# Renumbering the 128 slots of an expert's token tile: which partition holds which token

## The chip, the cores and the metric

The kernel runs on one core of one Trainium2 chip. The metric is device time in microseconds of one execution. Three runs of the kernel before took 906.35, 906.56 and 908.56 us, median 906.56.

## The reference

One decoder layer over 1024 tokens of width 1024, all float32: an input projection feeds sliding-window attention and latent attention, both go through one output projection, and a mixture of experts follows. What matters here is the last part:

```
expert_ids = g_idx * 8 + e_idx                      # best group of 4, best 2 of its 8 experts
combine    = weights placed at expert_ids           # (T, 32), two entries per token
hid = silu(x @ w_gate[e]) * (x @ w_up[e])           # for every expert e
hid = hid * combine[:, e]
out = sum over e of hid @ w_down[e]                 # then layer norm of ALPHA * h + out
```

So each of 1024 tokens goes to two of 32 experts: 2048 pairs, 64 an expert on average.

## The kernel before, in words

Everything up to the router runs in blocks of 128 tokens and ends at about 506 us of the span. The router (`route`) gives each pair of a token and an expert a running position p within that expert, in order of tokens. For a position below 128 it builds a one-hot row with `V.tensor_scalar(O, iota, pos[:, b, k:k + 1], None, op0=OP.is_equal)` (line 1529) and multiplies it on TensorE into a table `T` of 128 slots by 32 experts. So a pair with position p gets the slot s for which `iota[s] == p`. `finish_table` turns the table into `idxX` (the token's row for each slot, past the bound for an empty slot) and `wsl` (its weight). A slot is a partition of all the tiles that follow. Tile 24 in the order of work is an overflow tile, for an expert with more than 128 tokens, whose table `overflow_table` builds from the same `iota` (line 1843).

The expert stage then walks through 33 tiles of 128 slots. `gather_x` reads the 128 rows of a tile from `h1_d` by an indirect DMA of GpSimd (tile `w`), four tiles ahead of their use. `x_tr` transposes them on TensorE (`tr`), and `split` makes a high part on ScalarE (`xh`) and a low part on VectorE (`xl`). `gate_up` multiplies them by the expert's weights in four pieces (`gu`, three matmuls each: high by high, low by high, high by low), `hidden` makes `sil` and `hid`, `hid_tr` transposes and splits these (`hh`, `hl`), and `down` makes `y` in two halves, which ScalarE copies to a `w` tile. `scatter` adds its rows to `y_d` in DRAM by an indirect DMA of GpSimd with addition.

An expert's weights are three loads of 1024 KB each, 128 partitions of 8 KB, issued by SyncE into a ring of twelve buffers (tags `rw`, `rx`, `rv`, `rb`). A buffer comes free when `w_split` has made its two halves: `whg`, `whd` on ScalarE and `wlg`, `wld` on VectorE. `load_next` then issues the next load, so the ring holds the weights of four tiles.

After the last but two tiles the rows of `y_d` are read back (`z_load` by blocks, `old_rows` for the last two tiles by indirect DMA), normed and stored. `renorm` then writes the tokens of the last two tiles once more, by indirect DMA to the output.

The order of the instructions on each engine is set when the program is built: all operations are recorded, and `Sched.flush` puts them into order by a cost model of its own. Each engine works through its list in order. All operations are issued from one line, 312, so the names of tiles tell them apart in the profile.

Of the kernel before, what the change touches and what calls it, by code (L numbers as in the profile page):

```python
# [37 lines left out]
C_ID, C_TRI, C_IOTA, C_E32 = 0, 128, 256, 384  # L38
# [1933 lines left out]
def _constants():  # L1972
    import numpy as np
    c = np.zeros((128, C_END), np.float32)
    q = np.arange(128)[:, None]
    k = np.arange(128)[None, :]
    c[:, C_ID:C_ID + 128] = np.eye(128)
    cur = np.where(k <= q, 0.0, NEG)
    mask = np.concatenate([(k > q) & (k >= 128 - NMETA), cur, q > k, q <= k], axis=1).astype(np.float32)
    c[:, C_TRI:C_TRI + 128] = q < k  # L1980
    c[:, C_IOTA:C_IOTA + 128] = k % 8 * 16 + k // 8
    col = np.arange(512)[None, :]
    bd = ((q[:64] // NMETA) == (col // 128)).astype(np.float32)
    c[:, C_E32:C_E32 + 32] = np.arange(32)
    J, e = np.divmod(np.arange(224), 32)
    key = np.zeros((128, 2, 7, 32), np.float32)
    key[:, 0] = (32 * (J + 1) + e).reshape(7, 32)
    key[:, 1] = (128 * (J + 1)).reshape(7, 32)
    c[:, C_TOK:C_TOK + 8] = np.arange(128)[:, None] + 128 * np.arange(8)[None, :] - EMPTY
    c[:, C_WROW] = 3 * np.arange(128)  # L1990
    inv = 10000.0 ** (-np.arange(0, 64, 2, dtype=np.float32) / np.float32(64))
    pos = np.zeros((128, 9), np.float32)
    pos[:, :8] = NMETA + 128 * np.arange(8)[None, :] + np.arange(128)[:, None]
    pos[:, 8] = np.maximum(np.arange(128) - (128 - NMETA), 0)
    ang = (pos[:, :, None] * inv.astype(np.float32)[None, None, :]).astype(np.float32)
    rope = np.zeros((128, 9, 2, 64), np.float32)
    rope[:, :, 0, :32] = rope[:, :, 0, 32:] = np.cos(ang)
    rope[:, :, 1, :32] = -np.sin(ang)
    rope[:, :, 1, 32:] = np.sin(ang)
    return c, rope, bd, key, mask  # L2000
# [51 lines left out]
```

## Time and profile before

| | |
|---|---|
| median of three runs | 906.56 us |
| the profiled execution | 908.6 us |
| its span, first to last instruction | 906.7 us |
| TensorE busy | 802.8 us (89%) |
| VectorE busy | 686.1 us (76%) |
| ScalarE busy | 516.8 us (57%) |
| GpSimd busy | 310.6 us (34%) |
| queue of SyncE (hardware) | 36688 packets, 166.41 MB |
| queue of GpSimd (software) | 12816 packets, 28.87 MB |

A span is counted from the first instruction of the program, and all times below are on that clock. The expert stage lies between about 508 and 850 us. Busy shares are averages over stages with different limits, so the stage itself has to be read: the pace of its tiles, the time from a load's issue to its landing, and what stands ahead of each gap of TensorE. A load's landing is the time from the issuing instruction until the last of its sixteen engines has reported; with several loads in flight it holds the time in the queue too.

### The profile page before, as it was taken

Reading aid. Unit: us, or ns where it says so; the run is one execution under the profiler, and the core shown is the slowest. Engines: PE = TensorE matmul, PEld = TensorE weight load, DVE = VectorE, ACT = ScalarE, POOL = GpSimd, SP = SyncE. Lnnn points to the kernel's source line nnn. Section 1 sums busy time; section 2 is a strip of 40 time slices with the busy share of each in tenths; the row PEclk is TensorE's granted clock in tenths of the full one; section 3 lists DMA queues with packets and bytes.
Section 4 is the critical chain, followed back from the end, with each engine's and each line's share of the span. In section 5 each row is a group of like instructions: output and inputs, shape, how many; then the busy total and the mean of one; then the engine's idle time right before and its main releaser. Section 6 shows DMA issues by size and latency. Waiting matters only on the chain. (4 is left out here: it accounts for less than half of the span.)

```text
span 906.7 us, 13670 instructions
## 1 busy us (share of the span) xinstructions
PE 802.8 (89%) x4616; PEld 693.8 (77%) x4616; DVE 686.1 (76%) x1379; ACT 516.8 (57%) x966; POOL 310.6 (34%) x561
## 2 busy tenths in 40 slices
PE   3899999999999999999999599999999779989410
PEld 2798998999999988888887488888888658877310
DVE  7946623888777655758767799999999678979395
ACT  3524422576655645512122499999998578878351
POOL 3757423344331225223213414334343412321200
PEclk9999999999999999999999599999999979999855
DMA  9544512122211112699958469999999999994532
GB/s 333 173 152 160 177 68 92 35 87 69 84 51 47 48 70 70 218 343 411 350 170 308 150 222 362 353 373 370 354 356 329 357 328 346 366 317 131 177 141 105
DMA packets 49576, 196.17 MB, mean 216 GB/s; under 512 B 12688, under 2 KB 14224, under 8 KB 37344
## 3 DMA queue, kind: packets, MB, share of 16 engines
q1 hardware_dynamic: 36688, 166.41, 49.4%
q0 software_dynamic: 12816, 28.87, 11.5%
q8 instruction: 37, 0.61, 0.3%
q14 instruction: 35, 0.29, 0.1%
HBM read 165.57 MB, written 49.05 MB: 237 GB/s over the span
## 5 line engine op out<-in xcount | busy, mean ns | idle before, releaser
L312 POOL DMA_INDIRECT y_d<-w,idx x33 | 67.2, 2035 | 213.6 <-ACT w L312 184.7
L312 PE MATMUL sc<-wh,ht 128*128 128x448 f32 (+3 forms) x400 | 115.8, 370 | 1.9 <-DVE ht L312 1.3
L312 PE MATMUL gu<-whg,xh 128*128 128x512 f32 x264 | 110.2, 417 | 0.0
L312 PE MATMUL gu<-whg,xl 128*128 128x512 f32 x264 | 106.0, 402 | 0.7 <-DVE xl L312 0.7
L312 PE MATMUL gu<-wlg,xh 128*128 128x512 f32 x264 | 105.9, 401 | 0.0
L312 DVE TENSOR_TENSOR wlg<-rw,whg 128x1024 fp32r<-128x1024 f32 x80 | 96.4, 1221 | 12.3 <-ACT whg L312 11.7
L312 ACT ACTIVATE whg<-rw 128x1024 fp32r<-128x1024 f32 x80 | 83.8, 1062 | 23.4 <-PE gu L312 11.5
L312 PEld LDWEIGHTS sc<-wh,ht 128*128 128x128 f32 x400 | 73.8, 191 | 9.5 <-DVE ht L312 1.8
L312 PE MATMUL sc<-wl,ht 128*128 128x448 f32 (+3 forms) x200 | 72.8, 364 | 0.0
L312 PEld LDWEIGHTS gu<-whg,xl 128*128 128x128 f32 x264 | 50.9, 193 | 11.2 <-DVE xl L312 1.9
L312 DVE TENSOR_TENSOR wld<-rw,whd 128x1024 fp32r<-128x1024 f32 x46 | 54.4, 1221 | 6.5 <-ACT whd L312 6.4
L312 PEld LDWEIGHTS gu<-wlg,xh 128*128 128x128 f32 x264 | 50.7, 192 | 10.9
L312 PEld LDWEIGHTS gu<-whg,xh 128*128 128x128 f32 x264 | 51.1, 193 | 9.4 <-ACT xh L312 0.2
L312 PE MATMUL y<-whd,hh 128*128 128x512 f32 x124 | 52.0, 420 | 6.9 <-ACT hh L312 6.8
L312 POOL DMA_INDIRECT w<-h_d,idx x33 | 47.7, 1444 | 22.5 <-DMA y_d<-w,idx 11.0
L312 PE MATMUL tr<-cs,w 128*128 128x128 f32 x264 | 40.8, 279 | 12.9 <-DMA w<-h_d,idx 7.3
L312 PE MATMUL y<-whd,hl 128*128 128x512 f32 x124 | 50.2, 405 | 1.9 <-DVE hl L312 1.9
L312 PE MATMUL sc<-w,oT 128*128 128x512 f32 x192 | 49.8, 402 | 0.6 <-DMA oT<-o_d 0.6
L312 PEld LDWEIGHTS tr<-cs,w 128*128 128x128 f32 x264 | 33.6, 144 | 21.6 <-DVE wld L312 7.5
L312 PE MATMUL y<-wld,hh 128*128 128x512 f32 x124 | 49.6, 400 | 0.0
L312 ACT ACTIVATE pt<-sc,ng 128x272 f32<-128x272 f32 (+9 forms) x56 | 29.9, 538 | 34.5 <-DVE ng L312 34.3
L312 DVE TENSOR_TENSOR xl<-tr,xh 128x512 fp32r<-128x512 f32 x66 | 45.3, 687 | 3.9 <-ACT xh L312 3.7
(328 smaller groups left out, 2093.6 us busy)
## 6 DMA issues: line engine op xcount, KB each, us to landing
rw<-in_w_e_dram SPq DMA_DIRECT2D x64, 1024.0 KB, 24.5
rv<-in_w_e_dram SPq DMA_DIRECT2D x14, 1024.0 KB, 21.5
o_d<-oT SPq DMA_DIRECT2D x16, 512.0 KB, 2.8
oT<-o_d POOLq DMA_DIRECT2D x16, 512.0 KB, 8.5
rx<-in_w_e_dram SPq DMA_DIRECT2D x7, 1024.0 KB, 24.3
rb<-in_w_e_dram SPq DMA_DIRECT2D x7, 1024.0 KB, 26.2
x<-in_w_in_dram SPq DMA_DIRECT2D x8, 672.0 KB, 5.8
u_d<-r SPq DMA_DIRECT2D x7, 672.0 KB, 3.3
```

The source lines that it names most:

```text
L312: inst = getattr(t.eng.real, method)(*[self.real(a) for a in args], **{k: self.real(v) for k, v in kw.items()})
```

## The change

The 128 numbers of `iota` are permuted, and nothing else differs. Partition k stood for position k mod 8 x 16 + k div 8. Now it stands for the position whose lowest bit is bit 6 of k, whose bits 1 to 3 are bits 2 to 4 of k, whose bit 4 is bit 5 of k and whose bits 5 and 6 are bits 0 and 1 of k. Positions 0, 1, 2, 3 lay in partitions 0, 8, 16, 24; they lie in 0, 64, 4, 68 now. By the author's account partition bits 6 and 4 to 2 name a DMA engine, and successive rows are to lie on different engines.

```
@@ -1978,7 +1978,7 @@
     cur = np.where(k <= q, 0.0, NEG)
     mask = np.concatenate([(k > q) & (k >= 128 - NMETA), cur, q > k, q <= k], axis=1).astype(np.float32)
     c[:, C_TRI:C_TRI + 128] = q < k
-    c[:, C_IOTA:C_IOTA + 128] = k % 8 * 16 + k // 8
+    c[:, C_IOTA:C_IOTA + 128] = k // 64 + (k // 4 % 8) * 2 + (k // 32 % 2) * 16 + k % 4 * 32
     col = np.arange(512)[None, :]
     bd = ((q[:64] // NMETA) == (col // 128)).astype(np.float32)
     c[:, C_E32:C_E32 + 32] = np.arange(32)
```

On all five engines the instructions and their order are the same before and after. What differs is in the data: which slots of a tile are empty, and which partition a token's row is read into and added from.

## Rows read from the trace of the kernel before

**Rows 1.** Span and mean granted TensorE clock of the core.
```profile
core 0: 906.7 us, clock 0.948
```
**Rows 2.** Busy time by engine (PE, PEld, DVE, ACT, POOL), clock, DMA share, GB/s.
```profile
500.00:520.00 20.00, 8.72 (x30) 6.77 (x30) 15.22 (x47) 8.34 (x11) 9.77 (x8) 0.51 0.48 160
...
540.00:560.00 20.00, 20.00 (x99) 16.46 (x98) 19.43 (x22) 18.13 (x26) 7.45 (x5) 1.00 0.99 343
...
640.00:660.00 20.00, 20.00 (x100) 16.50 (x99) 19.83 (x25) 18.42 (x27) 9.13 (x5) 1.00 1.00 363
...
720.00:740.00 20.00, 12.48 (x47) 9.59 (x46) 11.43 (x14) 11.11 (x15) 6.37 (x5) 0.74 0.90 317
740.00:760.00 20.00, 16.99 (x76) 13.57 (x75) 14.89 (x17) 14.41 (x21) 3.44 (x3) 0.91 1.02 341
```
**Rows 3.** Issues at 526–537, 610–630, 685–705, 760–780: count, size, median us to landing.
```profile
rw<-in_w_e_dram SPq DMA_DIRECT2D x4, 1024.0 KB, 4.9
...
rw<-in_w_e_dram SPq DMA_DIRECT2D x4, 1024.0 KB, 23.2
...
rw<-in_w_e_dram SPq DMA_DIRECT2D x5, 1024.0 KB, 34.6
...
rw<-in_w_e_dram SPq DMA_DIRECT2D x4, 1024.0 KB, 25.1
```
**Rows 4.** ScalarE in order of time: start, us, operation, [idle before <- what ended it].
```profile
606.84 0.37 ACT L312 ACTIVATE sil<-gu 128x256 f32<-128x256 f32 x1
...
616.22 0.36 ACT L312 ACTIVATE sil<-gu 128x256 f32<-128x256 f32 x1
...
702.00 0.36 ACT L312 ACTIVATE sil<-gu 128x256 f32<-128x256 f32 x1
...
711.97 1.06 ACT L312 ACTIVATE whg<-rw 128x1024 fp32r<-128x1024 f32 x1 [2.66 <-DMA rw<-in_w_e_dram]
...
713.41 0.38 ACT L312 ACTIVATE sil<-gu 128x256 f32<-128x256 f32 x1
...
725.65 2.00 ACT L312 ACTIVATE whg<-rw 128x1024 fp32r<-128x1024 f32 x2 [6.17 <-DMA rw<-in_w_e_dram]
...
728.62 2.00 ACT L312 ACTIVATE whg<-rw 128x1024 fp32r<-128x1024 f32 x2 [0.70 <-DMA rw<-in_w_e_dram]
...
731.00 0.37 ACT L312 ACTIVATE sil<-gu 128x256 f32<-128x256 f32 x1
...
741.92 0.36 ACT L312 ACTIVATE sil<-gu 128x256 f32<-128x256 f32 x1
```
**Rows 5.** Waits, 520 to 800 us: total us, times, longest us.
```profile
ACT whg L312 <- DMA rw<-in_w_e_dram: 10.5, 4, 6.2
```
**Rows 6.** TensorE and ScalarE at two gaps of TensorE, as rows 4.
```profile
727.97 0.80 PE L312 MATMUL y<-whd,hh 128*128 128x512 f32 x1 [6.80 <-ACT hh L312]
...
747.46 0.66 PE L312 MATMUL tr<-cs,w 128*128 128x128 f32 x4 [2.87 <-DVE hl L312]
...
743.60 2.01 ACT L312 ACTIVATE whd<-rw 128x1024 fp32r<-128x1024 f32 x2
...
745.97 0.40 ACT L312 ACTIVATE hh<-tr 128x256 fp32r<-128x256 f32 x1
```
**Rows 7.** The same columns as rows 2, a stretch before the expert stage.
```profile
410.00:420.00 10.00, 10.00 (x66) 8.95 (x65) 8.12 (x34) 3.00 (x6) 2.96 (x10) 1.00 1.03 417
```
**Rows 8.** The first gather's landing, and the first transpose upon it.
```profile
w<-h_d,idx POOLq DMA_INDIRECT x1, 5.1
...
513.79 1.94 PE L312 MATMUL tr<-cs,w 128*128 128x128 f32 x8 [7.30 <-DMA w<-h_d,idx]
```
**Rows 9.** Landings of two late scatters, and the re-read of GpSimd behind the first.
```profile
y_d<-w,idx POOLq DMA_INDIRECT x1, 8.9
...
851.28 1.05 POOL L312 DMA_INDIRECT w<-y_d,idx  x1 [5.70 <-DMA y_d<-w,idx]
...
out_dram<-w,idx POOLq DMA_INDIRECT x1, 2.7
```

More of the change, by code (lines that the diff above doesn't have):

```diff
@@ L1980, in _constants @@
     c[:, C_TRI:C_TRI + 128] = q < k
-    c[:, C_IOTA:C_IOTA + 128] = k % 8 * 16 + k // 8
+    c[:, C_IOTA:C_IOTA + 128] = k // 64 + (k // 4 % 8) * 2 + (k // 32 % 2) * 16 + k % 4 * 32
     col = np.arange(512)[None, :]
```

## The prediction

> **What bounds the kernel now.** I read the span first [rows 1], then the expert stage in stretches of 20 us, then the landings of the weight loads there, then ScalarE's and TensorE's rows where TensorE stands still. In the stretches [rows 2] the pairs are busy microseconds and instruction counts of TensorE, its weight loads, VectorE, ScalarE and GpSimd; then come the granted clock, the DMA share and GB/s. From 540 to 680 TensorE is busy for 20.00 of 20 us at clock 1.00: the stage runs at TensorE's pace. A tile (one expert) takes 9.38 us there, from one `sil` to the next, 606.84 to 616.22 [rows 4]. But the DMA share is about 1.00 at some 360 GB/s, and behind this calm something runs out. A 1 MB weight load lands 4.9 us after its issue at 526 to 537, 23.2 us at 610 to 630, 34.6 us at 685 to 705, and 25.1 us at 760 to 780 [rows 3]. The twelve buffers hold four tiles, 4 x 9.38 = 37.5 us of work, so a landing of 34.6 us is the end of the cover. There ScalarE waits for `rw`: 2.66 us at 711.97, 6.17 at 725.65, 0.70 at 728.62 [rows 4], with one small wait more 10.5 us in four waits [rows 5]. It works in order, so the `hh` queued behind waits too, and TensorE loses 6.80 us before 727.97 [rows 6] and then its clock: 0.74 in 720 to 740, 0.91 in 740 to 760 [rows 2].
>
> So until 700 the stage is bound by TensorE, and its weight supply is slower than TensorE; about 710 to 742 it pays the debt.
>
> **The change, step by step.** No instruction is added, removed or moved; only the numbers in `iota` differ. They decide in which partition of a 128-slot tile an expert's p-th token lies, and so which partitions hold the real rows of each row gather and scatter-add; the empty slots have an index past the bound and move no row.
>
> *Step 1, the load on the DMA engines.* The change's own account takes a partition's bits 6 and 4 to 2 as the number of its DMA engine: sixteen engines, eight partitions each. The old numbering puts row p in partition (p mod 16) x 8 + p div 16. For p under 64 the last three bits are 0 to 3, so bit 2 is always 0: 64 rows lie on eight engines, eight on each, and the other eight engines get rows only from p = 64 on. The new numbering sends the low four bits of p to bits 6 and 4 to 2: 64 rows are four on each of sixteen. An expert gets 2048 / 32 = 64 rows on average; routing the reference's inputs gives 13 to 132. Summed over the first 20 tiles, the fullest engine has 6.7 rows a tile by the old numbering and 4.05 by the new one (mean 3.66).
>
> In bytes: a tile's weights are three loads of 1024 KB, 196.6 KB an engine. A row is 4 KB, moved once in and once out, 8.2 KB. The fullest engine has 196.6 + 6.7 x 8.2 = 251.5 KB a tile before and 196.6 + 4.05 x 8.2 = 229.8 after, 0.914 of it. If the adding scatter's read of its target counts too, 12.3 KB a row, it is 279.0 and 246.4, 0.883.
>
> *Step 2, the pace of the supply.* From the middle of 526 to 537 to that of 685 to 705 are 164 us, 17.5 tiles, and the landing grows by 34.6 - 4.9 = 29.7 us [rows 3], 1.7 us a tile. The crowded engines need 9.38 + 1.7 = 11.1 us a tile. As a check: eight engines at 251.5 KB per 11.1 us and eight at about 205 KB per 9.38 us are 181 + 175 = 356 GB/s, and the stretches show 343 and 363 [rows 2]. Afterwards 11.1 x 0.914 = 10.1, or x 0.883 = 9.8 us a tile; growth 0.4 to 0.8 us a tile. In 20 tiles the landing then reaches 13 to 20 us, in 32 tiles 18 to 29: under 34.6 throughout. No wait for weights is left, even if a third of the relief is missing.
>
> [...]
>
> *Step 3, what the waits were worth.* The three tile times that hold them are 702.00 to 713.41, to 731.00, to 741.92 [rows 4]: 11.41 + 17.59 + 10.92 = 39.92 us, against 3 x 9.38 = 28.14. That is 11.8 us, lost clock included. Bounds: 10.5 us if only ScalarE's waits go [rows 5]; nothing if the supply does not change; 14.7 if the 2.87 us gap at 747.46 goes as well [rows 6]. I take 11.8. That gap I leave standing: ahead of 747.46 TensorE waits for a transpose bank that is freed by `hh` and `hl`, and on ScalarE these stand behind two `whd` from 743.60, which run without a pause [rows 6]. It is the written order, no DMA, and the order stays. What is late next in 710 to 742 is TensorE itself, as in 540 to 680.
>
> *Step 4, the first gather.* It lands after 5.1 us and TensorE starts 513.79 upon it [rows 8]. The first tile has 66 rows: eight on a crowded engine before, at most five after. Three rows of 4 KB at 251.5 KB per 11.1 us are 0.5 us. Bounds: 0, if the clock, 0.51 in 500 to 520 [rows 2], rises no earlier; 2.4, if it lands like the 2.7 us scatter of 35 rows at the end [rows 9]. I take 0.5.
>
> *Step 5, the tail.* The scatter issued at 841.48 takes 8.9 us, and the re-read at 851.28 waits for it, 5.70 us of GpSimd's time [rows 9]. It has 93 rows, eight on an engine before and six after: two rows in and out at the same rate, 0.7 us; bounds 0 and 5.7. The last scatter [rows 9], of 35 rows, goes from five to three on an engine: 0.3 us at most. I take 0.7 for the two, since loads and VectorE's sums lie behind.
>
> *The hidden ones.* The other 32 gathers and 31 of the scatters land sooner as well, at no gain: a gather is issued four tiles ahead, and a `y_d` write is only read in the tail.
>
> Sum: 11.8 + 0.5 + 0.7 = 13.0 us. The profiled execution took 908.6 us (span 906.7), 2.0 over the median of the runs, 906.56. Against its own time the sum gives 895.6. If the 2.0 us is the profiled run's own, the median becomes 893.6; if it is a longer weight wait, which now goes, 895.6. I take **894.5**.
>
> **Rivals.**
>
> *A. It is the memory, not the engines.* If the 343 to 363 GB/s is what memory gives, all engines are slowed alike, evening them out does nothing, and steps 4 and 5 alone remain: 906.56 - 1.2 = 905.4. The same time comes if indirect rows are dealt by other bits, say partition modulo 16: the fullest engine then goes from 7.95 to 7.5 rows a tile, 0.1 us, 2 us in 20 tiles, 904.5. For it: the flat rate at a DMA share of 1.00. Against it: in 410 to 420, with whole 128-partition tiles only, the same core moves 417 GB/s at a share of 1.03 [rows 7]; and 66 rows, 0.27 MB, land in 5.1 us [rows 8] where a full 1 MB load with nothing queued before it takes 4.9 [rows 3], as rows crowded onto few engines would.
> [...]
>
> *B. Half.* The even load meets another limit on the way, and a tile's supply stays near 10.9 us. The landing grows 1.5 us a tile, the waits come three tiles later and half as long: 906.56 - 6 - 1 = 899.6. For it: the rate of the crowded engines, 251.5 KB per 11.1 us, is 22.7 GB/s, and sixteen at that rate are 362 GB/s, under the 417 of [rows 7], so something besides crowding slows them.
>
> *C. Slower.* If an indirect row's engine is its partition's block of eight (bits 6 to 3), the old numbering was the even one, 4.05 rows on the fullest engine, and the new one, whose bits 6 to 3 carry bits 0, 4, 3 and 2 of p, has 4.55. Half a row more is 4.1 KB of 229.8, 0.2 us of 11.1 a tile. At 711.97 the cover is spent, so every further microsecond of debt is waited for: 20 x 0.2 = 4 us, 910.6. It decides from 0.14 us a tile on (2.7 us). For it: nothing in the rows excludes an even load before. Against it: the same two points as against A.
>
> *D. More.* The two late gaps shrink too, since ScalarE comes to them earlier: 894.5 - 6 = 888.5. Against: at 743.60 it is the order that holds `hh` back.
>
> **How the numbers follow.** The forecast has 0.68 (its own range 890 to 898), A 0.08, B 0.12, C 0.06, D 0.06. The range 889 to 902 leaves out A, C, most of D and the upper end of B, under 2 in 10. About 0.3%, 2.7 us, is what a measurement of this kernel tells from no change: faster is under 903.8. That is the forecast, D and 0.10 of B: 0.84. The same: A and 0.02 of B, 0.10. Slower: C, 0.06.
>
> **What would show it.** Step 2: weight loads issued at 685 to 705 land in 13 to 20 us instead of 34.6, and GB/s in 640 to 660 rises from 363 to 364 to 375 (16 x 229.8 KB in 10.1 to 9.8 us). Step 3: no wait of ScalarE for `rw`, and `sil` rows 9.4 us apart through tiles 19 to 22, clock 1.00; the gap before the late transposes still there. Step 4: the first transpose at about 513.3. Step 5: the last big scatter in about 8 us. If landings still climb to 30 us, A or B is right; if they climb faster than 1.7 us a tile, C.

## The result, and the profile after

The kernel after takes 891.94 us (median of four runs, 891.67 to 893.8), the kernel before 906.72 us in the runs beside it (906.35 to 908.56): a ratio of 0.9837 with a 95% interval of 0.9818 to 0.9857, so faster by 1.6%. Forecast were 894.5 us in a range of 889 to 902. The profiled execution took 893.8 us with a span of 891.7, against 908.6 and 906.7 before [rows 1]: 15.0 us of span to be accounted for.

The span and the granted clock of the core, of the kernel after:

```profile
core 0: 891.7 us, clock 0.956
```

The stretches of the kernel after that answer to [rows 2], same columns (busy microseconds and instruction counts of TensorE, its weight loads, VectorE, ScalarE and GpSimd, then the granted clock, the DMA share and GB/s):

```profile
500.00:520.00 20.00, 8.81 (x28) 6.78 (x28) 15.65 (x47) 8.77 (x12) 9.48 (x8) 0.52 0.53 170
540.00:560.00 20.00, 20.00 (x102) 16.45 (x101) 19.41 (x22) 18.05 (x27) 7.31 (x4) 1.00 1.01 360
640.00:660.00 20.00, 20.00 (x102) 16.45 (x101) 19.82 (x25) 18.16 (x27) 8.82 (x6) 1.00 1.02 397
720.00:740.00 20.00, 17.65 (x80) 14.41 (x79) 15.92 (x18) 15.32 (x23) 6.64 (x5) 0.91 1.01 373
740.00:760.00 20.00, 20.00 (x101) 16.48 (x100) 19.15 (x21) 18.00 (x26) 6.40 (x4) 1.00 1.02 372
```

The DMA share stood at about 1.00 before and stands at 1.02 now; it does not tell the two kernels apart. The rate does: 397 GB/s in 640 to 660, where it was 363. One stretch alone can mislead (600 to 620 has 384 and 385), but the eight stretches from 540 to 700 average 384 GB/s, where they averaged 356. TensorE's 12.48 busy microseconds and clock of 0.74 in 720 to 740 have become 17.65 and 0.91, and the stretch after it is full.

The landings of the weight loads of the kernel after (tile, queue, kind, count, KB of one, median us from issue to landing), in the stretches 526 to 537, 570 to 590 (not among the rows before), 610 to 630, 685 to 705 and 760 to 780, which answer to [rows 3]:

```profile
rw<-in_w_e_dram SPq DMA_DIRECT2D x3, 1024.0 KB, 4.9
...
rw<-in_w_e_dram SPq DMA_DIRECT2D x5, 1024.0 KB, 8.1
...
rw<-in_w_e_dram SPq DMA_DIRECT2D x5, 1024.0 KB, 10.0
...
rw<-in_w_e_dram SPq DMA_DIRECT2D x5, 1024.0 KB, 10.8
...
rw<-in_w_e_dram SPq DMA_DIRECT2D x6, 1024.0 KB, 9.8
```

In the four stretches of [rows 3] they were 4.9, 23.2, 34.6 and 25.1 us. The first is the same; then the landing doubles to 10 us by 610 to 630 and climbs no further: from there on the loads keep up with TensorE.

ScalarE's rows of the kernel after (start, us, engine, line, operation, tiles, and in brackets the idle time before it with what ended it): the first `sil` of the stage, the four that bound the three tiles of step 3, the next one and the last of the stage, and between them the two `whg` in the places where the waits of 2.66 and of 6.17 us for weights had been:

```profile
525.16 0.39 ACT L312 ACTIVATE sil<-gu 128x256 f32<-128x256 f32 x1
...
701.21 0.36 ACT L312 ACTIVATE sil<-gu 128x256 f32<-128x256 f32 x1
...
708.22 1.06 ACT L312 ACTIVATE whg<-rw 128x1024 fp32r<-128x1024 f32 x1 [0.27 <-PE gu L312]
...
710.30 0.37 ACT L312 ACTIVATE sil<-gu 128x256 f32<-128x256 f32 x1
...
715.01 2.06 ACT L312 ACTIVATE whg<-rw 128x1024 fp32r<-128x1024 f32 x2
...
720.42 0.37 ACT L312 ACTIVATE sil<-gu 128x256 f32<-128x256 f32 x1
...
728.59 0.39 ACT L312 ACTIVATE sil<-gu 128x256 f32<-128x256 f32 x1 [0.47 <-PE gu L312]
...
743.19 0.36 ACT L312 ACTIVATE sil<-gu 128x256 f32<-128x256 f32 x1
...
832.55 0.38 ACT L312 ACTIVATE sil<-gu 128x256 f32<-128x256 f32 x1 [2.39 <-PE gu L312]
```

The three tiles take 9.09 + 10.12 + 8.17 = 27.38 us, where they took 39.92 [rows 4]: 12.5 us less. The first `whg` waits 0.27 us, for TensorE's `gu` and not for a load; the second, where the 6.17 us had been, waits for nothing. The first and the last `sil` of the kernel before, in the same columns:

```profile
526.02 0.38 ACT L312 ACTIVATE sil<-gu 128x256 f32<-128x256 f32 x1
...
845.96 0.38 ACT L312 ACTIVATE sil<-gu 128x256 f32<-128x256 f32 x1 [2.39 <-PE gu L312]
```

So from the first to the last `sil` the stage takes 307.4 us where it took 319.9, 12.5 us less, and it is all in those three. Up to the first `sil` the kernel after is 0.9 us ahead, and from the last `sil` to the end it takes 59.1 us instead of 60.7, 1.6 less. 0.9 + 12.5 + 1.6 = 15.0.

The waits of the kernel after in 520 to 800 (engine, what waits, for what: us in total, times, longest), which answer to [rows 5]:

```profile
ACT whg L312 <- PE gu L312: 18.9, 55, 1.5
...
POOL y_d L312 <- DMA rw<-in_w_e_dram: 5.7, 1, 5.7
```

No wait of ScalarE for `rw` is among them; GpSimd waits for `rw` twice, 5.7 and 1.7 us, but from 540 to 800 TensorE is busy for less than 20.00 us only in the two stretches with its late gaps. TensorE's two late gaps are still there, as the prediction left them; the first answers to the second gap of [rows 6]:

```profile
734.27 1.12 PE L312 MATMUL tr<-cs,w 128*128 128x128 f32 x4 [2.35 <-DVE hl L312]
...
785.57 1.09 PE L312 MATMUL tr<-cs,w 128*128 128x128 f32 x4 [2.69 <-DVE xl L312]
```

The second of the kernel before:

```profile
798.83 0.63 PE L312 MATMUL tr<-cs,w 128*128 128x128 f32 x4 [2.69 <-DVE xl L312]
```

The tile that holds the first of them takes 14.60 us (728.59 to 743.19), before 14.52 (741.92 to 756.44). Part of that is the clock, 0.52 in 734 to 736 and 0.62 in 736 to 738: in the kernel below whose scatter does not add, with the same order of instructions, the clock in 720 to 740 is 1.00 where this one's is 0.91, and the same tile takes 13.07 us (727.14 to 740.21), with TensorE busy for 17.66 of the 20 us there, as here for 17.65.

The start and the tail, which answer to [rows 8, 9]: TensorE's first transposes of the stage, GpSimd's re-read behind the last big scatter, and VectorE's sum behind the re-read, of the kernel after:

```profile
512.70 1.94 PE L312 MATMUL tr<-cs,w 128*128 128x128 f32 x8 [6.50 <-DMA w<-h_d,idx]
...
837.13 1.05 POOL L312 DMA_INDIRECT w<-y_d,idx  x1 [4.96 <-DMA y_d<-w,idx]
...
844.41 1.29 DVE L312 TENSOR_TENSOR w<-y,w 128x512 f32<-128x512 f32 x2 [10.95 <-DMA w<-y_d,idx]
```

The same sum of the kernel before:

```profile
859.27 1.29 DVE L312 TENSOR_TENSOR w<-y,w 128x512 f32<-128x512 f32 x2 [12.40 <-DMA w<-y_d,idx]
```

VectorE's wait there is 1.45 us shorter, GpSimd's (5.70 before) 0.74. The landings of the first gather and of the last big scatter, of the kernel after (5.1 and 8.9 us before):

```profile
w<-h_d,idx POOLq DMA_INDIRECT x1, 4.3
...
y_d<-w,idx POOLq DMA_INDIRECT x1, 8.2
```

### The profile page after: what moved, and what is told of

Same layout as the page of the kernel before. It is cut to its first block, busy times and chain, and to the rows that moved or that the text cites. A ratio compares the mean times of both kernels' runs of the same rounds, so it can differ in the third digit from the quotient of the medians.

```text
span 891.7 us, 13670 instructions
## 1 busy us (share of the span) xinstructions
PE 797.6 (89%) x4616; PEld 690.1 (77%) x4616; DVE 685.9 (77%) x1379; ACT 517.1 (58%) x966; POOL 312.5 (35%) x561
## 5 line engine op out<-in xcount | busy, mean ns | idle before, releaser
L312 ACT ACTIVATE whg<-rw 128x1024 fp32r<-128x1024 f32 x80 | 83.9, 1063 | 12.8 <-PE gu L312 11.1
L312 PEld LDWEIGHTS gu<-wlg,xh 128*128 128x128 f32 x264 | 50.5, 191 | 11.1
```

Source lines behind the costliest of these rows:

```text
L312: inst = getattr(t.eng.real, method)(*[self.real(a) for a in args], **{k: self.real(v) for k, v in kw.items()})
```

## The experiments

The theory: an indirect row is moved by the engine that bits 6 and 4 to 2 of its partition name, as the change's own account has it, and what the fullest engine has to move in a tile sets how fast the weights land. No trace names the engine of a row: below, an engine is the one that a row is counted to by these bits, and the weights are counted as 196.6 KB on every engine, an estimate from three loads of 1024 KB over sixteen; times and landings test the count. The rivals are that the engine is named by other bits (the block of eight, the partition modulo 16), another reason (it is not the number of rows on an engine that counts but that successive rows lie on different engines), and that a row costs its two moves but not a read of the target by the adding scatter.

The rows on the fullest engine are counted by the theory from the routing of the reference's inputs, per tile over the first 20 tiles. All kernels of the table but the last differ in the numbering alone; the edits below are shown against the kernel after, where no heading says otherwise:

```
kernel                       rows/tile   us       ratio to before, interval
after                        4.05        891.94   0.9837  0.9818 to 0.9857
even, other block of eight   4.05        890.49   0.9820  0.9798 to 0.9841
eleven engines               5.60        891.46   0.9819  0.9791 to 0.9847
quads on one engine          5.65        892.36   0.9835  0.9814 to 0.9855
before                       6.70        906.7 to 907.9 in three sets
identity                     7.15        912.23   1.0054  1.0037 to 1.0070
engine by engine             8.00        920.32   1.0151  1.0130 to 1.0171
before, scatter without add  6.70        893.72   0.9848  0.9819 to 0.9877
```

The rows/tile put the seven numberings in order: flat up to 5.65, and rising from somewhere below 6.70. The last line has the rows of the kernel before and the time of the even ones; it is taken up below.

**The identity.** Slot k holds position k.

```
-    c[:, C_IOTA:C_IOTA + 128] = k // 64 + (k // 4 % 8) * 2 + (k // 32 % 2) * 16 + k % 4 * 32
+    c[:, C_IOTA:C_IOTA + 128] = k
```

> Numbering with position p in partition p. Theory (the engine of an indirect row is bits 6 and 4 to 2 of its partition, and a crowded engine delays the weight loads): the fullest engine has 7.15 rows a tile over the first 20 tiles (before 6.70, after 4.05), so at least 0.65 us a row gives a supply of some 11.4 us a tile; landings climb faster than before, waits for rw start earlier; 0.3 us more in each of some 28 tiles, 915 us (911 to 918). Rival (engine = partition modulo 16): 4.05 rows on the fullest, even, as fast as after, 892 us. Rival (engine = block of eight partitions): 8.00 rows against 4.05 before, over 920 us, with the kernel after at 4.55 a little slower than before, which it was not.

Measured: 912.23 us (911.97 to 912.74), before beside it 907.29; ratio 1.0054 (1.0037 to 1.0070). The weight loads of 610 to 630 and of 640 to 660, and ScalarE's waits for them in 520 to 900, all of the kernel with the identity:

```profile
rw<-in_w_e_dram SPq DMA_DIRECT2D x5, 1024.0 KB, 28.4
...
rw<-in_w_e_dram SPq DMA_DIRECT2D x4, 1024.0 KB, 32.9
```

```profile
ACT whg L312 <- DMA rw<-in_w_e_dram: 17.3, 5, 6.1
```

The landings climb faster than before (28.4 us where 23.2 stood), and the waits are 17.3 us instead of 10.5. By the partition modulo 16 this numbering would have been an even one; that rival falls. By the block of eight it has 8.00 rows on the fullest engine and the kernel before 4.05, so that it should be as slow as the kernel filled engine by engine below, which has 8.00 by either count (920.32 us), and the kernel before as fast as the even ones; that falls too.

**An even load by the bits, with another block of eight.** The low four bits of the position still go to bits 6 and 4 to 2, but within an engine's eight partitions bits 0 and 1 are filled before bit 5, so that by blocks of eight the rows crowd.

```
-    c[:, C_IOTA:C_IOTA + 128] = k // 64 + (k // 4 % 8) * 2 + (k // 32 % 2) * 16 + k % 4 * 32
+    c[:, C_IOTA:C_IOTA + 128] = k // 64 + (k // 4 % 8) * 2 + k % 2 * 16 + (k // 2 % 2) * 32 + (k // 32 % 2) * 64
```

> Numbering whose four low bits name partition bits 6 and 4 to 2 as in the kernel after, but which fills bits 0 and 1 before bit 5. Theory: 4.05 rows on the fullest engine as after, landings at 685 to 705 about 11 us, 892 us (890.5 to 893.5). Rival (block of eight): 6.75 rows on the fullest, as crowded as before by bits 6 and 4 to 2; landings climb as before, 906 us. Rival (modulo 16): 5.50, between the two, about 895 to 900 us.

Measured: 890.49 us (889.34 to 891.78); ratio 0.9820 (0.9798 to 0.9841), the kernel after's within the interval. Its weight loads of 640 to 660 and of 685 to 705:

```profile
rw<-in_w_e_dram SPq DMA_DIRECT2D x5, 1024.0 KB, 11.0
...
rw<-in_w_e_dram SPq DMA_DIRECT2D x5, 1024.0 KB, 9.5
```

About level, as in the kernel after (10.8 us at 685 to 705). The order in which an engine's eight partitions are filled made no difference here, 890.49 us against 891.94 with overlapping intervals; the block of eight falls for good.

For indirect rows, in tiles about half of whose slots are empty here, the two runs agree with the count by bits 6 and 4 to 2: 912.23 us with 7.15 rows a tile against 890.49 with 4.05.

**Engine by engine.** The first eight positions go to one engine, the next eight to the next, and so on: the worst that these bits allow.

```
-    c[:, C_IOTA:C_IOTA + 128] = k // 64 + (k // 4 % 8) * 2 + (k // 32 % 2) * 16 + k % 4 * 32
+    eng = 8 * (k[0] >> 6) + ((k[0] >> 2) & 7)
+    c[:, C_IOTA + np.argsort(eng, kind="stable")] = k
```

> Numbering that fills the eight partitions of one engine, then of the next. Theory: 8.00 rows a tile on the first engines, 1.3 more than before; at 0.65 us a row a supply of about 12.0 us a tile. The cover of some 30 us is gone after 11 to 12 tiles, from then on the stage runs at the supply: 28 tiles x 0.85 us = 24 us over before, 930 us (922 to 938). Rival (something other than the count of rows on the fullest engine, say that any unevenness costs the same): about 907 us.

Measured: 920.32 us (919.4 to 922.18); ratio 1.0151 (1.0130 to 1.0171). The direction is as expected, the slowest of all; the size is a miss, under the 922 at which the expected range began. Its weight loads of 570 to 590, and ScalarE's waits in 520 to 900:

```profile
rw<-in_w_e_dram SPq DMA_DIRECT2D x5, 1024.0 KB, 21.3
```

```profile
ACT whg L312 <- DMA rw<-in_w_e_dram: 23.8, 9, 5.9
```

The loads land after 21.3 us where the kernel after has 8.1, and the waits come to 23.8 us. What failed is the price of a row, expected at 0.65 us, and with it the time at which the cover is gone: 11 to 12 tiles were expected, which end at some 635 us, and in 640 to 660 TensorE is still busy for 20.00 us (clock 0.97), in 685 to 705 for 15.70. All but 1.5 us of the waits come before 800 us, as do all of the identity's, and the last one of the kernel before up to there ends at 728.62, in its 22nd tile. Over 22 tiles the fullest engine has 176 rows here, 150 before and 159 with the identity. (920.3 - 907.3) / (176 - 150) is 0.50 us a row, and the identity's (912.2 - 907.3) / (159 - 150) is 0.54; over 23 tiles (184, 157 and 167 rows) it is 0.48 and 0.49.

**Quads on one engine.** Positions 0 to 3 lie on one engine, the next four on the next: successive rows share an engine, but 64 rows are spread over all sixteen.

```
-    c[:, C_IOTA:C_IOTA + 128] = k // 64 + (k // 4 % 8) * 2 + (k // 32 % 2) * 16 + k % 4 * 32
+    c[:, C_IOTA:C_IOTA + 128] = k % 4 + (k // 64) * 4 + (k // 4 % 8) * 8 + (k // 32 % 2) * 64
```

> Four successive rows lie on one engine, the next four on the next; 64 rows are still four on each of sixteen. Theory (the total on the fullest engine counts, not that neighbours lie apart): 5.65 rows on the fullest over the first 20 tiles, a supply of about 10.4 us a tile, landings of 20 to 25 us at 685 to 705, under the cover of 34.6, so no wait before 742 and 892 to 895 us; by tile 32 the landing may touch the cover. Rival (successive rows have to lie on different engines, as the change's name says): landings climb as before, about 906 us.

Measured: 892.36 us (891.2 to 893.59); ratio 0.9835 (0.9814 to 0.9855), as fast as the kernel after. So it is not what the change's own account says, that successive rows lie on different engines: it is the sum of rows on an engine, and 5.65 a tile, at 892.36 us, is still little enough. The profile of this run does not tell the landings, so that the 20 to 25 us expected there are not shown.

**Eleven engines.** Positions are dealt in turn to eleven of the sixteen engines until these are full.

```
-    c[:, C_IOTA:C_IOTA + 128] = k // 64 + (k // 4 % 8) * 2 + (k // 32 % 2) * 16 + k % 4 * 32
+    eng = 8 * (k[0] >> 6) + ((k[0] >> 2) & 7)
+    nth = (k[0] >> 5 & 1) * 4 + (k[0] & 3)
+    turn = eng % 8 * 2 + eng // 8
+    c[:, C_IOTA + np.lexsort((turn, nth, turn >= 11))] = k
```

> Rows are dealt in turn to eleven engines, the other five get rows only when these are full. The fullest has 188 rows over 32 tiles, as with the quads (189), but eleven engines stand near it (165 to 188), where the quads have four over 165. Theory (the fullest engine alone sets a load's landing): as the quads, 892 us. Rival (crowded engines also slow each other): on the line through before and the two slower numberings, 0.35 us a row, 907.3 - 31 x 0.35 = 896.4 us.

Measured: 891.46 us (890.94 to 891.88); ratio 0.9819 (0.9791 to 0.9847). Its weight loads of 526 to 537, 570 to 590, 610 to 630, 640 to 660, 685 to 705 and 760 to 780:

```profile
rw<-in_w_e_dram SPq DMA_DIRECT2D x4, 1024.0 KB, 5.0
...
rw<-in_w_e_dram SPq DMA_DIRECT2D x4, 1024.0 KB, 10.8
...
rw<-in_w_e_dram SPq DMA_DIRECT2D x4, 1024.0 KB, 15.1
...
rw<-in_w_e_dram SPq DMA_DIRECT2D x6, 1024.0 KB, 19.0
...
rw<-in_w_e_dram SPq DMA_DIRECT2D x6, 1024.0 KB, 24.9
...
rw<-in_w_e_dram SPq DMA_DIRECT2D x5, 1024.0 KB, 25.4
```

The time is the theory's 892 and not the rival's 896.4. This is the clearest of the runs. The supply is slower than TensorE, by (24.9 - 5.0) / 17.5 = 1.1 us a tile, and the landing climbs to 25 us; but the twelve buffers cover 37.5, and the kernel is as fast as one whose landings are flat. These landings cost nothing, since the cover was not spent. For the same reason its time can't show whether crowded engines also slow each other: the landing stays under the cover, and the quads give no landing to set beside it.

**The kernel before, with a scatter that doesn't add.** The old numbering stays, and the sum over the experts is left out.

```
...
-                             bounds_check=NB * 128 - 1, oob_is_err=False, compute_op=OP.add)
+                             bounds_check=NB * 128 - 1, oob_is_err=False)
```

> The numbering of the kernel before; the scatter writes its rows to y_d without adding them, which leaves out the sum over experts. Theory in the form that the read of the target counts as a third 4 KB on a crowded engine: 6.7 x 4.1 = 27.5 of 279.0 KB go, a supply of 10.0 us a tile instead of 11.1, landings of about 15 us at 685 to 705, no wait before 742, some 895 us. In the form that only in and out count (8.2 KB a row, 0.35 us, as the slope of the two slower numberings has it): nothing changes, 906 to 908 us.

Measured: 893.72 us (892.91 to 894.63) against 907.85 of the kernel before beside it; ratio 0.9848 (0.9819 to 0.9877). Its weight loads of 610 to 630 and of 685 to 705:

```profile
rw<-in_w_e_dram SPq DMA_DIRECT2D x5, 1024.0 KB, 11.4
...
rw<-in_w_e_dram SPq DMA_DIRECT2D x6, 1024.0 KB, 13.0
```

With the crowded numbering and the same count of rows, the weights land after 13.0 us instead of 34.6: taking the addition away brings the landing down about as far as spreading the rows does (10.8 us). So of step 1's two forms the one without the read, 8.2 KB a row, falls: by it nothing would have changed. The time agrees with the other, 12.3 KB a row (895 us expected), but that what the addition costs an engine is the read of the target is not shown; no run tells it apart from the adding itself.

**The planner's rate, with the new numbering.** The two late gaps are in the written order. The planner that writes it models every DMA at 372 GB/s. By this rate, so I read it, weights come late in two of the last third of the tiles, and it puts other work ahead of theirs. Here it is told 400 GB/s for the expert stage, near the 397 measured; nothing else is changed.

```
-        self.late, self.eager = 0.0, False
+        self.late, self.eager, self.rate = 0.0, False, 372e3
...
-            t.idx, t.late = len(self.tasks), self.late
+            t.idx, t.late, t.rate = len(self.tasks), self.late, self.rate
...
-                    t.end = self.transfer(t.end + 0.65, t.dma / 372e3) + 0.75
+                    t.end = self.transfer(t.end + 0.65, t.dma / t.rate) + 0.75
...
     ap.close()
+    sched.rate = 400e3
```

> The numbering of the kernel after; the planner's model of the DMA rate goes from 372 to 400 GB/s for the expert stage alone, so its order no longer puts the two token transposes of tiles 22 and 27 behind each other and behind the down products. Theory (the two late gaps are written into the order, no DMA ends them): the gaps of 2.35 and 2.69 us and the half clock after them go, the two tiles fall from 14.6 and 14.1 us to 9.4: 10 us off 891.9, 882 us (880 to 885). Rival (the gaps are waits for something that arrives late): the gaps stay or reappear elsewhere, 890 to 893 us.

Measured: 882.24 us (881.57 to 882.7); ratio 0.9718 (0.9695 to 0.9742), the best of all, 9.7 us under the kernel after. The stretches of this kernel where the late gaps had been, and its `sil` rows there:

```profile
720.00:740.00 20.00, 20.00 (x99) 16.43 (x98) 19.41 (x23) 18.32 (x27) 7.33 (x4) 1.00 1.03 375
...
780.00:800.00 20.00, 20.00 (x100) 16.43 (x99) 19.40 (x22) 18.32 (x27) 7.08 (x4) 1.00 0.83 296
```

```profile
718.84 0.37 ACT L312 ACTIVATE sil<-gu 128x256 f32<-128x256 f32 x1
728.23 0.36 ACT L312 ACTIVATE sil<-gu 128x256 f32<-128x256 f32 x1
737.61 0.36 ACT L312 ACTIVATE sil<-gu 128x256 f32<-128x256 f32 x1
746.99 0.37 ACT L312 ACTIVATE sil<-gu 128x256 f32<-128x256 f32 x1
```

TensorE is busy throughout at clock 1.00, and the tiles are 9.38 us apart.

**The planner's rate, with the old numbering.** The same edit, and the same order of instructions, with the old `iota` line.

> The same order as e5 with the numbering of the kernel before. Theory (with crowded engines the stage is bound by the supply of weights, and the two gaps repay part of the debt for nothing): the gaps go, but waits for rw grow by as much, and the time stays at 905 to 908 us. Rival (the order and the numbering are worth the same apart as together): 10 us off as in e5, 897 us.

Measured: 910.48 us (ten runs, 908.91 to 911.57) against 907.85; ratio 1.0034 (1.0018 to 1.0049). No gain, as expected, and some 2.5 us more than the range allowed. ScalarE's waits for `rw` in 520 to 800, the landings of 610 to 630 and 685 to 705, and two late rows of ScalarE, of this kernel:

```profile
ACT whg L312 <- DMA rw<-in_w_e_dram: 10.9, 6, 2.6
```

```profile
rw<-in_w_e_dram SPq DMA_DIRECT2D x3, 1024.0 KB, 21.3
...
rw<-in_w_e_dram SPq DMA_DIRECT2D x5, 1024.0 KB, 33.6
```

```profile
804.02 2.00 ACT L312 ACTIVATE whg<-rw 128x1024 fp32r<-128x1024 f32 x2 [3.85 <-DMA rw<-in_w_e_dram]
...
826.22 1.06 ACT L312 ACTIVATE rw<-rw 128x1024 fp32r<-128x1024 f32 x1 [10.13 <-DMA rw<-in_w_e_dram]
```

The order without gaps asks for weights that are not there: the landing is at 33.6 us again, ScalarE waits 10.9 us up to 800, 5.3 more from there to 814 (3.85 of it at 804.02) and another 10.13 at 826.22. In one order the numbering is worth 14.8 us (906.7 to 891.9), in the other 28.2 (910.5 to 882.2). Why the sum lies 2.6 us over the kernel before, and not at it, was not taken apart.

## Why the prediction was right

*What bounds the kernel.* Right: an expert stage at TensorE's pace whose supply of weights falls behind under it, and a debt paid at 710 to 742 when the cover of four tiles is spent. The eleven engines show the cover by itself, 25 us of landing at no cost.

*Step 1, the engine of a row.* Right in effect. No row of a profile names the engine that moved an indirect row; the bits are inferred from seven numberings whose times follow the count by them, and from the fall of the two other maps. Of the two forms, 8.2 or 12.3 KB a row, the scatter without the add rules out 8.2 and agrees with 12.3: 246.4 against 279.0 KB, 0.883.

*Step 2, the pace of the supply.* The direction was right, the size too careful. Forecast were landings of 13 to 20 us at 685 to 705, for relief by 12.3 and by 8.2 KB a row; measured were 10.8. The end at 20 us falls with the smaller form. Of the larger form's 13, part was my counting: 20 tiles of growth, where the two stretches are 17.5 tiles apart. Over these it gives 9.8 - 9.38 = 0.42 us a tile and 4.9 + 17.5 x 0.42 = 12.2 us, against 0.34 a tile measured. What failed is the shape. A steady climb was forecast; the landing reaches 8.1 us at 570 to 590 and 10.0 at 610 to 630 and then stays, so the supply keeps up with the tiles from there on, and the rate in 640 to 660 is 397 GB/s and not 364 to 375. At 9.38 us a tile the weights and the rows moved in and out, without a read of the target by the adding scatter, come to 16 x (196.6 + 3.66 x 8.2) KB / 9.38 us = 387 GB/s, and the eight stretches from 540 to 700 average 384: the stage gets what it takes at TensorE's pace.

In proportion to bytes a row of 12.3 KB should cost 12.3 KB x 11.1 us / 279.0 KB = 0.49 us a tile. The whole kernels give 0.50 to 0.54 us. The landings give more at first: from 526 to 537 to 610 to 630, 9.5 tiles, they grew by 1.06 us a tile with 5.5 rows on the fullest engine in the first ten tiles (eleven engines), 1.93 with 6.6 (before) and 2.48 with 7.1 (identity), or 0.8 to 1.1 us a row; but by 0.54 with 3.9 (the kernel after), only 0.3 us a row from there to the eleven engines. Over the 17.5 tiles to 685 to 705 it is 0.5 us a row again: 0.34 us a tile with 4.05 rows, 1.14 with 5.60, 1.70 with 6.70, though the kernel before has waited 0.94 us at 691.00 by then, so that its landing may be held back by the cover. So the price by the landings depends on the stretch, and why a row costs about twice as much by it in the first ten tiles stays open. None of this touched the forecast time, since the landing, forecast and measured, lies far under the cover.

*Step 3, the waits.* 11.8 us forecast, 12.5 measured on the same three tiles. The 0.7 us more is that the three now take 27.38 us, less than the 28.14 of three tiles at 9.38: the written order moves some of the work between neighbours (9.09, 10.12, 8.17), which the waits had covered. The two late gaps stayed, as forecast: the first went from 2.87 to 2.35 us without a shorter tile (14.60 us against 14.52), and the second is 2.69 in both. So rival D, that they shrink as ScalarE comes sooner, falls, and the planner's rate shows what they are: order, worth 9.7 us once the weights are there in time.

*Step 4, the first gather.* 0.5 us forecast. TensorE's wait for it was 7.30 us before [rows 8] and is 6.50 after, 0.8 less. The other kernels repeat it: 7.20 with the identity, 7.05 engine by engine, 7.21 and 7.16 in the other two with the old numbering, against 6.55 and 6.47 in the other two even ones; quads and eleven engines lie between, at 6.72 and 6.88. The first `sil` itself comes at 525.2 instead of 526.0, but it stands at 523.5 and 523.8 in the two other kernels with the old numbering, so that of the 0.9 us of span at the start only the wait's share can be credited to the change.

*Step 5, the tail.* 0.7 us forecast, 1.6 measured: too small, well inside its bounds of 0 and 5.7. Of GpSimd's wait 0.74 us went, which was the forecast's reason. What I left out is that the re-read behind it is an indirect gather as well, of the same slots, and is spread by the same change: VectorE's wait for it went from 12.40 to 10.95 us. It is 11.0 and 10.7 in the two other even kernels, 12.0 in the other old one with the add, 12.0 and 12.5 with the identity and engine by engine.

*The rivals.* A (memory) falls by the 397 GB/s and by the time; 905.4 was its price. The partition modulo 16, put beside A at 0.1 us a tile and 904.5, is 0.16 us by the same sum (0.45 x 8.2 of 261.8 KB, 11.1 us), so 3 us in 20 tiles and 903.4; it falls by the identity, 912.23. B (half, 899.6) falls since the landing is flat. Its ground was 22.7 GB/s an engine, counted at 8.2 KB a row, the form that fell; at 12.3 KB the crowded engines had 279.0 KB per 11.1 us, 25.1 GB/s by this estimate, and sixteen such are 402, near the 417 of [rows 7]. C (slower by the block of eight) falls by the second experiment.

The sum was 13.0 us against 15.0 of span. The choice between the profiled run's 2.0 us over the median as its own or as a longer wait, taken halfway at 894.5, mattered as much as any small step: the kernel after's profiled run, too, lies 1.9 us over its median.

## What to carry to other kernels

Where rows are gathered or scattered into tiles that are only partly full, count the rows that fall on each DMA engine by the partition they lie in, weights and all, and compare the fullest engine's load with the time of a tile; the mean over the engines hides it (here 3.66 rows a tile in both kernels, 6.70 and 4.05 on the fullest engine by the count, 906.72 and 891.94 us). A landing that climbs through a stage is a debt: with eleven engines it climbed to 25.4 us under a cover of 37.5 and cost nothing (891.46 us), in the kernel before it reached 34.6 us at 685 to 705, and three tiles took 39.92 us instead of 28.14. So read the trend and the cover together. After such a repair look at what was written for the slower supply: the planner's 372 GB/s was worth 9.7 us more once it no longer described the core.

## What was not expected of the hardware

- The addition in the scatter costs time beyond the move of the rows: dropping the addition alone, with the rows as crowded as before, took the landing at 685 to 705 from 34.6 to 13.0 us and the time from 907.85 to 893.72.
- A DMA share of about 1.00 goes with 363 GB/s and crowded engines as with 397 GB/s and even ones (640 to 660): it didn't tell the two kernels apart.
- The load did not have to be even here. 4.05 and 5.65 rows a tile on the fullest engine give the same time within the intervals (891.94 and 892.36 us); 6.70 costs 15 us.
